# Two stores cut into 112 + 8 + 8 rows to shift packets between DMA engines, with a target for each waiting copy

## The chip, the cores and the metric

One core of one Trainium2 chip runs the kernel. The metric is device time in microseconds (us), the median of several executions. A profile of one execution is about 1.8 us shorter than the time, because it starts with the first instruction and ends with the last (before: 128.05 us for an execution with a span of 126.2 us).

## The reference

Linear attention with ReLU features: batch 8, 12 heads (96 heads in all), 512 positions, 64 dimensions, fp32.

```python
Q_feat, K_feat = np.maximum(0, Q), np.maximum(0, K)
KV = np.einsum('bhkd,bhkv->bhdv', K_feat, V)
K_sum = np.sum(K_feat, axis=2)
numerator = np.einsum('bhqd,bhdv->bhqv', Q_feat, KV)
denominator = np.einsum('bhqd,bhd->bhq', Q_feat, K_sum)
out = numerator / (denominator[:, :, :, None] + 1e-10)
```

Three inputs of 12.6 MB are read and one output of 12.6 MB is written; there is little arithmetic.

## The kernel before

The kernel works in 12 "octets" of eight heads. GpSimd issues the loads of K, V and Q ahead, two K and two V tiles and one Q tile per octet, cast to bf16 on the way (octet 0's K and V come uncast, from SP and ScalarE). SP issues the stores, one of 1 MB (128 partitions x 8 KB) per octet, and holds each of the first seven back with a tiny copy that must wait for a K tile five octets ahead: so loads go before stores. The last octet's store is cut into two halves by columns.

```python
    scratch = consts.tile([1, D], bf16, name="scratch")
    ...
    def store(o, o_sb):
        if o + DELAY < NO:                      # NO = 12, DELAY = 5
            nc.sync.dma_start(out=scratch, in_=k_sb[2 * (o + DELAY)][0:1, 0, :])
        parts = 2 if o == NO - 1 else 1
        n = RQ // parts
        for j in range(parts):
            rs = slice(n * j, n * (j + 1))
            nc.sync.dma_start(out=Or[o].rearrange("p (r d) -> p r d", d=D)[:, rs], in_=o_sb[:, rs])
    ...
    for o in range(NO + 1):                     # cut: matmuls, evacuations and preparation
        if o > 0:
            mm_out(o - 1, 2)
            norm(o - 1, 2, o_sb)
            store(o - 1, o_sb)
```

## Time and profile before

| | before |
|---|---|
| time, median of the first three runs | 127.86 us (127.86 to 128.26) |
| span of the profiled execution | 126.2 us |
| DVE, ACT, PE busy | 64%, 61%, 61% |
| DMA engines | 90% or more in 38 of 40 slices |
| last landing of the last store, per engine | eight at 122.8 to 124.0, eight at 124.6 to 125.3 us |
| last store issued | 120.05 us |

How to read it: no compute engine is near its limit, the DMA engines are. Each store of 128 rows raises its semaphore 16 times (13 of 13 stores in this trace), read here as once for each of the 16 DMA engines: while the last eight landings are still out, the DMA share is 0.46 (124.0 to 124.5 us), about eight engines of 16. So a transfer's sixteen landings in the trace show how far apart the engines are, though not which engine is which. The lines of the page and of the tail's windows are in the prediction.

### The profile page before, as it was taken

Reading aid. Unit: us, or ns where it says so; the run is one execution under the profiler, and the core shown is the slowest. Engines: PE = TensorE matmul, PEld = TensorE weight load, DVE = VectorE, ACT = ScalarE, POOL = GpSimd, SP = SyncE. Lnnn points to the kernel's source line nnn. Section 1 sums busy time; section 2 is a strip of 40 time slices with the busy share of each in tenths; the row PEclk is TensorE's granted clock in tenths of the full one; section 3 lists DMA queues with packets and bytes.
Section 4 is the critical chain, followed back from the end, with each engine's and each line's share of the span. In section 5 each row is a group of like instructions: output and inputs, shape, how many; then the busy total and the mean of one; then the engine's idle time right before and its main releaser. Section 6 shows DMA issues by size and latency. Waiting matters only on the chain.

```text
span 126.2 us, 4865 instructions
## 1 busy us (share of the span) xinstructions
PE 77.3 (61%) x2112; PEld 68.3 (54%) x2112; DVE 80.6 (64%) x210; ACT 76.9 (61%) x169; POOL 32.1 (25%) x62
## 2 busy tenths in 40 slices
PE   0032917978397956534997647389964793797200
PEld 0041907967386845434986646178953692696100
DVE  3256785698936959673669787528828628774900
ACT  0165891599198798660799949508917925958000
POOL 6902424325243331241143133033113000000000
PEclk9999999999859999996799999955999679769995
DMA  3999999999999999999999999999999999999992
GB/s 106 374 309 213 214 208 209 217 206 218 205 215 209 208 214 324 257 216 325 256 215 301 280 214 281 301 212 214 347 235 216 316 266 216 352 418 410 416 384 104
DMA packets 10757, 32.81 MB, mean 260 GB/s; under 512 B 1392, under 2 KB 1392, under 8 KB 9328
## 3 DMA queue, kind: packets, MB, share of 16 engines
q0 software_dynamic: 8064, 17.83, 73.9%
q1 hardware_dynamic: 2384, 13.63, 27.1%
q10 hardware_dynamic: 288, 1.05, 2.1%
q8 instruction: 16, 0.26, 0.7%
q14 instruction: 5, 0.04, 0.1%
HBM read 37.75 MB, written 12.58 MB: 399 GB/s over the span
## 4 chain that ended last, share of the span: by engine, by line
DMA 32%; PE 27%; issue 13%; ACT 11%; DVE 10%; ACTq 1%; SPq 0%
DMA v_sb<-in_V_dram 25%; PE ps_out L174 13%; PE ps_kv L139 11%; DMA kv_first<-in_K_dram 7%; ACT kvd L146 5%; ACT qt L159 4%; PE ps_qt L153 3%; DVE o_sb L187 3%; DVE qt L121 3%; ACT vo L134 3%; DVE kf L128 2%; DVE vo L130 1%; DVE rec L186 1%; ACTq L267 0%; DVE kvd L118 0%
## 5 line engine op out<-in xcount | busy, mean ns | idle before, releaser
L139 PE MATMUL ps_kv<-vo,kf 128*128 128x130 bf16 x384 | 32.5, 248 | 21.9 <-ACT vo L134 11.7
L174 PE MATMUL ps_out<-kvd,qt 128*32 128x130 bf16 x1536 | 33.7, 243 | 16.7 <-issue 13.3
L139 PEld LDWEIGHTS <-kf 128*128 128x128 bf16 x384 | 27.8, 112 | 25.3 <-DVE vo L130 16.3
L174 PEld LDWEIGHTS <-qt 128*32 128x32 bf16 x1536 | 27.0, 107 | 21.9 <-issue 15.3
L146 ACT CAST kvd<-ps_kv 64x130 bf16<-64x130 f32 x96 | 25.2, 263 | 16.7 <-PE ps_kv L139 14.8
L134 ACT ACTIVATE vo<-v_sb,mask 128x1024 bf16<-128x1024 bf16 x22 | 26.2, 1190 | 13.9 <-DMA v_sb<-in_V_dram 13.8
L187 DVE TENSOR_TENSOR o_sb<-ps_out,rec 128x768 f32<-128x768 f32 (+1 forms) x36 | 31.3, 868 | 1.4
L159 ACT ACTIVATE qt<-ps_qt 128x512 bf16<-128x512 bf16 x48 | 24.8, 603 | 0.3
L128 DVE TENSOR_SCALAR kf<-k_sb,mask 128x1024 bf16<-128x1024 bf16 x44 | 19.1, 476 | 8.6 <-DMA k_sb<-in_K_dram 8.6
L85 POOL DMA_DIRECT2D k_sb<-in_K_dram x22 | 12.8, 583 | 39.1 <-DMA q_sb<-in_Q_dram 24.1
L184 DVE TENSOR_SCALAR den<-ps_out 128x12 f32<-128x12 f32 (+1 forms) x36 | 5.9, 164 | 17.9 <-PE ps_out L174 17.8
L153 PE MATMUL ps_qt<-ident,q_sb 128*128 128x128 bf16 x192 | 15.7, 245 | 2.4 <-issue 2.4
L87 POOL DMA_DIRECT2D v_sb<-in_V_dram x22 | 12.3, 557 | 17.1 <-DMA k_sb<-in_K_dram 7.3
L153 PEld LDWEIGHTS <-q_sb 128*128 128x128 bf16 x192 | 14.0, 112 | 2.6 <-issue 2.5
L130 DVE TENSOR_SCALAR vo<-v_sb,mask 128x1024 bf16<-128x1024 bf16 x22 | 10.6, 481 | 2.1 <-DMA v_sb<-in_V_dram 2.1
L186 DVE RECIPROCAL rec<-den 128x12 f32<-128x12 f32 (+1 forms) x36 | 7.9, 220 | 1.2
L91 POOL DMA_DIRECT2D q_sb<-in_Q_dram x12 | 6.5, 542 | 7.8 <-DMA v_sb<-in_V_dram 4.1
L128 DVE TENSOR_SCALAR kf<-kv_first,mask 128x1024 bf16<-128x1024 f32 x4 | 2.8, 750 | 4.9 <-DMA kv_first<-in_K_dram 4.9
L134 ACT ACT_TABLE_LOAD x1 | 1.3, 1283 | 5.8 <-DMA kv_first<-in_V_dram 5.8
L121 DVE MEMSET qt<- 128x2048 f32 x2 | 3.5, 1765 | 0.8 <-issue 0.8
L134 ACT ACTIVATE vo<-kv_first,mask 128x1024 bf16<-128x1024 f32 x2 | 2.4, 1180 | 2.6 <-DMA kv_first<-in_V_dram 2.6
L130 DVE TENSOR_SCALAR vo<-kv_first,mask 128x1024 bf16<-128x1024 f32 x2 | 1.5, 747 | 0.0
(12 smaller groups left out, 3.5 us busy)
## 6 DMA issues: line engine op xcount, KB each, us to landing
out_dram<-o_sb SPq DMA_DIRECT2D x11, 1024.0 KB, 9.2
q_sb<-in_Q_dram POOLq DMA_DIRECT2D x12, 512.0 KB, 14.9
k_sb<-in_K_dram POOLq DMA_DIRECT2D x22, 256.0 KB, 13.8
v_sb<-in_V_dram POOLq DMA_DIRECT2D x22, 256.0 KB, 13.2
kv_first<-in_V_dram ACTq DMA_DIRECT2D x2, 512.0 KB, 7.3
kv_first<-in_K_dram SPq DMA_DIRECT2D x2, 512.0 KB, 7.0
out_dram<-o_sb SPq DMA_DIRECT2D x2, 512.0 KB, 5.1
scratch<-k_sb SPq DMA_DIRECT2D x7, 0.1 KB, 5.1
```

Source lines behind the costliest of these rows:

```text
L85: nc.gpsimd.dma_start(out=k_sb[g].rearrange("p r d -> p (r d)"), in_=Kr[g])
L87: nc.gpsimd.dma_start(out=v_sb[g].rearrange("p r d -> p (r d)"), in_=Vr[g])
L128: nc.vector.tensor_scalar(kf[g][:, :, s, :], k_sb[g], scalar1=0.0, scalar2=mask[:, 0, s:s + 1], op0=Alu.max, op1=Alu.mult)
L130: nc.vector.tensor_scalar(vo[g % NB][:, :, 0, 0:D], v_sb[g], scalar1=mask[:, 1, 0:1], scalar2=None, op0=Alu.mult)
L134: nc.scalar.activation(vo[g % NB][:, :, 1, 0:D], v_sb[g], Act.Copy, scale=mask[:, 1, 1:2])
L139: nc.tensor.matmul(ps_kv[g], kf[g][:, r, :, :].rearrange("p s d -> p (s d)"), vo[g % NB][:, r, :, :], start=(r == 0), stop=(r == R - 1), s ...
L146: nc.scalar.copy(kvd[g % NK][64 * c:64 * c + 64, :, s, c, :], ps_kv[g][64 * s:64 * s + 64])
L153: nc.tensor.transpose(ps_qt[o, i][:, u, :], q_sb[o][:, i * (U // 2) + u, :], ident)
L159: nc.scalar.activation(qtz[o % NZ][:, z, us, :, z, :], pv[:, :, :, z, :], Act.Relu)
L174: nc.tensor.matmul(po[hs, b, c:c + 2 * D1], qtf[o % NZ][:, z, u * P + 32 * w:u * P + 32 * w + 32], kvd[(2 * o + h // 4) % NK][:, h % 4 // ...
L186: nc.vector.reciprocal(rec, den)
L187: nc.vector.tensor_tensor(o_sb[:, 2 * u0:2 * (u0 + nu)].rearrange("p (b r) d -> p b r d", b=2), pv[:, :, :, 0:D], rec.unsqueeze(3).to_broa ...
```

## The change

Intent: the DMA engines don't end together, so two stores are cut such that eight engines carry a packet more each per store and eight one less. The tiny waiting copies get a target each, and in octets 0 to 3 there is a second one that waits for a V tile.

```diff
-    scratch = consts.tile([1, D], bf16, name="scratch")
+    scratch = consts.tile([1, 2 * NO, D], bf16, name="scratch")
...
+    def cuts(o):
+        rows = slice(0, RQ)
+        if o in (1, 3):
+            return [(slice(0, 112), rows), (slice(112, 120), rows), (slice(120, P), rows)]
+        if o == NO - 1:
+            return [(slice(0, P), slice(0, RQ // 2)), (slice(0, P), slice(RQ // 2, RQ))]
+        return [(slice(0, P), rows)]
...
     def store(o, o_sb):
-        if o + DELAY < NO:
-            nc.sync.dma_start(out=scratch, in_=k_sb[2 * (o + DELAY)][0:1, 0, :])
-        (one or two stores by columns)
+        n = 2 * (o + DELAY)
+        if n < 2 * NO:
+            for x, i in ((v_sb, n - 1), (k_sb, n))[0 if o < 4 else 1:]:
+                nc.sync.dma_start(out=scratch[:, i], in_=x[i][0:1, 0, :])
+        Ov = Or[o].rearrange("p (r d) -> p r d", d=D)
+        for ps, rs in cuts(o):
+            nc.sync.dma_start(out=Ov[ps, rs], in_=o_sb[ps, rs])
```

More of the change, by code (lines that the diff above doesn't have):

```diff
@@ L190, in norm @@
             rec.unsqueeze(3).to_broadcast([P, 2, nu, D]), op=Alu.mult)
-    def store(o, o_sb):
-        if o + DELAY < NO:
-            nc.sync.dma_start(out=scratch, in_=k_sb[2 * (o + DELAY)][0:1, 0, :])
-        parts = 2 if o == NO - 1 else 1
-        n = RQ // parts
-        for j in range(parts):
-            rs = slice(n * j, n * (j + 1))
-            nc.sync.dma_start(out=Or[o].rearrange("p (r d) -> p r d", d=D)[:, rs], in_=o_sb[:, rs])
+    def cuts(o):
[5 more added lines that the diff above has]
+        return [(slice(0, P), rows)]
+    def store(o, o_sb):
+        n = 2 * (o + DELAY)
[5 more added lines that the diff above has]
+            nc.sync.dma_start(out=Ov[ps, rs], in_=o_sb[ps, rs])
     zero(0)
```

## The prediction

The text calls eight engines "0 to 7" and the other eight "8 to 15". Take the numbers as names for two groups: those on which a transfer of 8 rows lands, and the rest. That both pieces of 8 rows take the same eight engines, one row each, was taken for granted when it was written. The trace of the kernel after agrees with it: the 112 rows of octet 1 land 16 times (61.00 to 62.63 us), the two pieces eight times each (61.59 to 63.05 and 62.21 to 63.67 us; in order, the second's are 0.50 to 0.68 us behind the first's), besides one landing each 0.44 to 0.48 us after the issue.

> **What bounds the kernel now.** I read the page first for the share of each engine, then its DMA lines, then the windows of the last stretch, and last the landings of single transfers in the trace.
>
> The busiest compute engine (DVE) is busy for 64% of the span. The DMA lines read otherwise:
>
> ```profile
> DMA  3999999999999999999999999999999999999992
> DMA packets 10757, 32.81 MB, mean 260 GB/s; under 512 B 1392, under 2 KB 1392, under 8 KB 9328
> q0 software_dynamic: 8064, 17.83, 73.9%
> q1 hardware_dynamic: 2384, 13.63, 27.1%
> q8 instruction: 16, 0.26, 0.7%
> HBM read 37.75 MB, written 12.58 MB: 399 GB/s over the span
> ```
>
> Thirty-eight of forty slices have the 16 DMA engines at 90% or more, and the queues' shares sum to 103.9% (packets overlap a little at their ends). So the transfers set the time: the kernel ends when the DMA engines have worked off their packets. The last line says how much: 50.3 MB. The q8 line will matter: 16 packets of 0.26/16 MB = 16 KB each, instruction fetches, and each runs on one engine alone.
>
> The question for this change is whether all 16 engines finish together. The windows of the tail answer it (columns: window, its length, busy time and count of PE, PEld, DVE, ACT, POOL, then granted clock, DMA share, GB/s):
>
> ```profile
> 118.00:120.00 2.00, 0.36 (x28) 0.18 (x15) 1.90 (x4) 0.00 (x0) 0.00 (x0) 1.00 0.98 403
> 121.00:122.00 1.00, 0.00 (x0) 0.00 (x0) 0.00 (x0) 0.00 (x0) 0.00 (x0) 1.00 1.03 426
> 122.00:122.50 0.50, 0.00 (x0) 0.00 (x0) 0.00 (x0) 0.00 (x0) 0.00 (x0) 1.00 0.90 361
> 122.50:123.00 0.50, 0.00 (x0) 0.00 (x0) 0.00 (x0) 0.00 (x0) 0.00 (x0) 0.76 0.68 279
> 123.00:123.50 0.50, 0.00 (x0) 0.00 (x0) 0.00 (x0) 0.00 (x0) 0.00 (x0) 0.50 0.63 254
> 123.50:124.00 0.50, 0.00 (x0) 0.00 (x0) 0.00 (x0) 0.00 (x0) 0.00 (x0) 0.50 0.52 213
> 124.00:124.50 0.50, 0.00 (x0) 0.00 (x0) 0.00 (x0) 0.00 (x0) 0.00 (x0) 0.50 0.46 188
> 124.50:125.00 0.50, 0.00 (x0) 0.00 (x0) 0.00 (x0) 0.00 (x0) 0.00 (x0) 0.50 0.09 33
> ```
>
> Compute is over at about 120 us. The DMA share is full until 122, then falls to a plateau of about one half from 123.5 to 124.5, then to nothing: about half the engines run out of work some 2 us before the rest. The trace's landings say it per engine: every store raises its semaphore 16 times, once per engine. For the last half store these times are 122.76, 122.79, 122.81, 122.83, 122.94, 123.41, 123.53, 123.97, and then 124.56, 124.93, 124.95, 124.97, 124.99, 125.08, 125.10, 125.28. Eight engines are early (mean 123.1), eight late (mean 125.0): a gap of 1.9 us. The cause fits q8. Its packets start at 25.0, 31.4, 37.4, 43.4, 49.6, 56.0, 62.1, 68.1, 74.1 and so on to 118.6 us and take 0.88 to 0.98 us. In the loads' landings one more engine falls behind after each of the first eight; from the ninth on an engine already behind falls behind a second time (the K tile landing at 76.5 has a single engine 1 us behind the next). So the same eight engines fetch twice: 2 x 0.94 = 1.9 us, the gap.
>
> How much could balancing give at most? The missing share from 122.0 to 124.87, where the last packet ends: 0.5 x (0.10 + 0.32 + 0.37 + 0.48 + 0.54) + 0.37 x 0.88 = 1.2 us. No perfect split of the same work gives more than about 1.2 us, or 1% of 127.86.
>
> [...]
>
> **The change part by part.**
>
> 1. *Octets 1 and 3 as 112 + 8 + 8.* Engines 8 to 15 go from 8 packets to 7, engines 0 to 7 to 7 + 1 + 1 = 9. Over two octets: two packets fewer on one half, two more on the other. A packet of 8 KB: in the tail, where only stores run, one engine's landings of successive 1 MB stores are 2.45 us apart (fastest engine 112.55, 114.99, 117.44), so 2.45 / 8 = 0.306 us. The shift is 0.61 us each way, 1.22 us of the 1.9 us gap, if engines 8 to 15 are the late ones. The extra pieces add two completion packets per octet on engines 0 to 7, about 20 ns each in the trace: under 0.1 us in all. The extra issues cost SP about 0.5 us each (the issues' median is 0.53); SP waits some 9 us per octet for the next K tile, so that is hidden.
>
> 2. *Four more waiting copies (V tiles, octets 0 to 3).* V tile 2(o+5)-1 is loaded ahead of the K tile that SP waits for anyway, and lands earlier: tile 9 lands at 39.36, K tile 10 at 42.86. No store goes out later for it, beyond an issue of 0.5 us that lies in the wait for K. But each copy is split into 16 packets of 8 bytes (112 of them for seven copies in the trace, median 22 ns) with a completion each of about 20 ns: some 0.05 us of every engine per copy, 0.2 us for four at most, an estimate.
>
> 3. *A target for each copy.* The chain on SP's queue before:
>
> ```profile
> SPq L197 <- DMA k_sb<-in_K_dram: 71.9, 7, 41.3
> SPq L197 <- DMA scratch<-k_sb: 22.8, 6, 4.3
> SPq L202 <- DVE o_sb L187: 9.0, 4, 5.9
> ```
>
> SP waits 22.8 us in all for the earlier copy, because all copies write one target. But a copy lands about 5 us after its issue (47.99 for the one of 42.88) and the next K tile lands at 52.9: the wait for the copy ends first and that for K ends last. Removing it starts no store earlier. Worth 0.
>
> Sum: the late engines end at 125.28 - 0.61 + 0.2 = 124.9; the early ones at latest 123.97 + 0.61 + 0.2 + 0.1 = 124.9. The two halves meet, 0.4 us sooner. The compute tail (last store issued at 120.05, earliest landing 122.76) leaves room, and loads on the late engines land a little earlier, so it doesn't take over. 127.86 - 0.4 = 127.46, said as **127.5 us**.
>
> **Rivals.**
>
> - *The wrong half.* Nothing in this trace names an engine. If the eight late ones are 0 to 7, the change adds to them: 125.28 + 0.61 + 0.2 + 0.1, a time near 128.8. For the right half speaks only that the diff was evidently drawn for this imbalance: two packets are the shift that closes most of the gap, three would overshoot. I give the wrong half 1 in 8.
> - [...]
> - *Nothing moves.* Balance is given back by another engine's lateness: the time is the maximum of 16, and the three middle ones (123.41 to 123.97) lie in the half that gets more. Then 127.7 to 127.9. The three times of before (127.86 to 128.26) spread by as much as the expected gain.
>
> **Range and chances.** The main case (two in three) gives 127.2 to 127.7; a failed half[...] 128 to 129.5. Range 127.0 to 128.7. Faster by over 2% needs 125.3 us, twice the 1.2 us that perfect balance could give: 1%. Slower by over 2% needs 130.4[...]: 3%. The rest is within 2%: 96%.
>
> **What would show it.** Right: the last transfer's sixteen landings within about 0.7 us instead of 2.5, the DMA share near 1 until about 124 and then falling at once with no plateau at one half; the split octets' last pieces land eight times; last landing 124.7 to 125.0. SP's wait for an earlier copy gone, its wait for K and V tiles as long as both before, stores issued at the same times (43.5, 53.5, 63.5). Wrong: a gap near 3 us at the end (wrong half); [...] or 8-byte packets that cost much more than 22 ns. The prediction fails as a whole if the DMA share has dips in mid-kernel that it has not now.

## The result, and the profile after

The changed kernel took 128.11 us (127.97 to 128.47, 6 runs) against 128.02 us (127.86 to 128.26, 6 runs) for the kernel before: ratio 1.0013, 95% interval 0.9994 to 1.0032. In a second set of runs, with the experiments, it was 0.9999 (0.9984 to 1.0013). So the time stayed, and the forecast gain of 0.4 us did not come.

The page of the kernel after, in the lines that answer to those of before:

```profile
DMA  3999999999999999999999999999999999999992
DMA packets 10917, 32.82 MB, mean 260 GB/s; under 512 B 1552, under 2 KB 1552, under 8 KB 9488
q0 software_dynamic: 8064, 17.83, 73.9%
q1 hardware_dynamic: 2544, 13.63, 27.1%
q8 instruction: 16, 0.26, 0.7%
```

There are 160 more packets, all under 512 bytes (64 of 8 bytes, and 96 completions: 64 of the copies, 32 of the extra pieces), and no measurable time in them: q1 takes 27.1% as before. The tail's windows, columns as before (window, length, five engines, granted clock, DMA share, GB/s):

```profile
121.00:122.00 1.00, 0.00 (x0) 0.00 (x0) 0.00 (x0) 0.00 (x0) 0.00 (x0) 0.78 0.99 410
122.00:122.50 0.50, 0.00 (x0) 0.00 (x0) 0.00 (x0) 0.00 (x0) 0.00 (x0) 0.50 0.96 393
122.50:123.00 0.50, 0.00 (x0) 0.00 (x0) 0.00 (x0) 0.00 (x0) 0.00 (x0) 0.50 1.05 426
123.00:123.50 0.50, 0.00 (x0) 0.00 (x0) 0.00 (x0) 0.00 (x0) 0.00 (x0) 0.50 0.81 328
123.50:124.00 0.50, 0.00 (x0) 0.00 (x0) 0.00 (x0) 0.00 (x0) 0.00 (x0) 0.50 0.68 279
124.00:124.50 0.50, 0.00 (x0) 0.00 (x0) 0.00 (x0) 0.00 (x0) 0.00 (x0) 0.50 0.23 90
124.50:125.00 0.50, 0.00 (x0) 0.00 (x0) 0.00 (x0) 0.00 (x0) 0.00 (x0) 0.50 0.12 49
```

Read the DMA share, the last column but one. The plateau at one half is gone: the share is high until 123 and down to 0.23 at 124. But then it does not end. From 124.5 to 125 it is 0.12, and 0.12 x 16 is two engines. The landings of the last store in the trace say the same (us):

```
before  122.76 .79 .81 .83 .94 123.41 .53 .97 | 124.56 .93 .95 .97 .99 125.08 .10 .28
after   123.49 .56 .58 .61 .69 124.05 .19 .43 .46 .47 .63 .69 .73 .89 | 125.40 .43
```

Fourteen engines are now within 1.4 us of each other, which is the balance that was meant, and two come 0.5 us behind all others. The kernel waits for those two. A second profiled execution of the changed kernel, taken with the experiments, shows the same with three: thirteen engines by 124.47, then 125.20, 125.22 and 125.55.

SP's waits in the kernel after (engine and line, what it waited for, us in total, times, longest):

```profile
SPq L210 <- DMA k_sb<-in_K_dram: 45.6, 7, 9.0
SPq L210 <- DMA v_sb<-in_V_dram: 45.4, 4, 38.3
SPq L278 <- DMA out_dram<-o_sb: 3.8, 3, 1.4
```

The wait for an earlier copy (22.8 us before) is gone, and the waits for K and V tiles took its place. The first three stores go out when they did: 43.6, 53.7, 63.6 us against 43.5, 53.5, 63.5.

### The profile page after: what moved, and what is told of

Same layout as the page of the kernel before. It is cut to its first block, busy times and chain, and to the rows that moved or that the text cites. A ratio compares the mean times of both kernels' runs of the same rounds, so it can differ in the third digit from the quotient of the medians.

```text
span 126.3 us, 4883 instructions
## 1 busy us (share of the span) xinstructions
PE 77.8 (62%) x2112; PEld 68.8 (54%) x2112; DVE 80.8 (64%) x210; ACT 77.2 (61%) x169; POOL 31.4 (25%) x62
## 3 DMA queue, kind: packets, MB, share of 16 engines
q1 hardware_dynamic: 2544, 13.63, 27.1%
## 4 chain that ended last, share of the span: by engine, by line
PE 42%; DMA 21%; issue 17%; DVE 9%; ACT 4%; ACTq 1%; SPq 0%
PE ps_out L174 18%; PE ps_kv L139 18%; DMA v_sb<-in_V_dram 14%; DMA kv_first<-in_K_dram 7%; PE ps_qt L153 6%; DVE qt L121 3%; ACT kvd L146 2%; DVE o_sb L187 2%; DVE kf L128 2%; ACT qt L159 1%; ACT vo L134 1%; DVE vo L130 1%; ACTq L278 1%; DVE rec L186 1%; DVE kvd L118 0%
## 5 line engine op out<-in xcount | busy, mean ns | idle before, releaser
L139 PE MATMUL ps_kv<-vo,kf 128*128 128x130 bf16 x384 | 33.7, 252 | 22.1 <-ACT vo L134 10.5
L139 PEld LDWEIGHTS <-kf 128*128 128x128 bf16 x384 | 28.3, 113 | 25.7 <-DVE vo L130 15.6
L184 DVE TENSOR_SCALAR den<-ps_out 128x12 f32<-128x12 f32 (+1 forms) x36 | 6.0, 166 | 22.9 <-PE ps_out L174 22.8
```

Of the source, the lines that this page charges most:

```text
L139: nc.tensor.matmul(ps_kv[g], kf[g][:, r, :, :].rearrange("p s d -> p (s d)"), vo[g % NB][:, r, :, :], start=(r == 0), stop=(r == R - 1), s ...
```

## The experiments

The theories: **A**, the late engines are just engines 8 to 15 and the gain was eaten by something else (packets, compute); **B**, the late engines are a mixed set, so that a cut by engine number makes some late ones later; **C**, it was the wrong half. Beside them stood the rival: slow packets in the small stores. The first two kernels measure which engines are late; then each part of the change runs alone; the other eight runs test what the findings predict, one of them being the changed kernel once more.

### Which engines are late: probes in both kernels

In the traces a transfer of 8 or 4 rows lands as often as it has rows, read here as on as many engines: the pieces of 8 rows eight times (above), the 8-row probe below eight times, the 4-row probe four times, each time 0.18 to 0.19 us behind a landing of the 8-row probe, so on four of the same engines. No trace numbers them: "0 to 7" are the eight of the one, "0 to 3" the four of the other, "8 to 15" the rest. That pieces and probe take the same eight is the assumption; the landings of the two pieces (above) and the shift measured below (1.3 us, 1.22 worked out) agree with it. So tiny copies behind octet 9's store report when their engines are done with it, 0.2 us later (below). The same edit was made to both kernels:

```diff
+    probe = consts.tile([16, 8, D], bf16, name="probe")
+    # behind octet 9's store
+    for i, n in enumerate((8, 4, 12, 6, 10)):
+        nc.sync.dma_start(out=probe[0:n, i], in_=ident[0:n, 0:D])
```

> A measuring kernel: the kernel before, with five tiny probe copies (8, 4, 12, 6 and 10 rows) issued right behind octet 9's store. [...] Theory A (the eight late engines are exactly 8 to 15): all eight landings of the 8-row probe lie in the early group (about 117.4 to 119.1 us), and the 12-row probe adds four late ones (near 120.0). Theory B (the late eight are a mixed set): the 8-row probe has one to three landings near 120.0 among the early ones. Theory C (wrong half): all eight near 120.0. Time at most 0.5 us over before.

Measured in the kernel before (one execution, 128.15 us, state unknown, so only the order of the engines is used):

```
store of octet 9, 16 engines   117.45 .49 .53 .81 118.02 .55 .58 119.07 | 119.21 .60 120.03 .04 .06 .08 .11 .12
probe of 8 rows (engines 0-7)  117.68 .69 .99 118.73 .77 119.40 .81 120.29
probe of 4 rows (engines 0-3)  117.88 118.18 .92 .95
```

The 8-row probe was issued first; matched in order, each of its landings is 0.2 us behind one of the store's. Less 0.2, engines 0 to 7 read 117.5, 117.5, 117.8, 118.5, 118.6, 119.2, 119.6 and 120.1: the last three are among the store's eight late landings. The 4-row probe has none of the late. So five late engines are in 8 to 15, three are in 4 to 7, and three engines of 8 to 15 are early. Theory B. (The landings of the other three probes are left out. They fit this map but for one of the 12-row probe, at 119.45, which has no store landing 0.2 us before it. The eighth and ninth landings of the store, 119.07 and 119.21, are close, so it may be the ninth that belongs to engines 8 to 15: then six late ones are there and two in 4 to 7. The set is mixed either way.)

> The same five probes in the changed kernel. Octet 9's store there lands in three groups in the profile: two early (117.1, 117.5), twelve between 118.1 and 119.8, two late (120.5). Theory B (mixed set): the two late landings belong to engines 0 to 7 (they are in the 8-row probe), which were late before and were given two packets more, and the two earliest to engines 8 to 15 (not in the 8-row probe). Theory D (something random, such as one more fetch, made two engines late): the two latest need not be among 0 to 7.

In the changed kernel (one execution, 128.71 us, state unknown):

```
store of octet 9, 16 engines   116.81 117.22 | 117.86 118.10 .11 .57 .78 119.01 .02 .16 .24 .27 .32 .47 | 120.16 .59
probe of 8 rows (engines 0-7)  118.07 .29 .76 .97 119.21 .67 120.37 .80
```

Less 0.2, the 8-row probe ends with 120.17 and 120.60: the two latest engines are both in 0 to 7. It begins with 117.87: the two earliest are both in 8 to 15. That is what moving packets from one half to the other does to a mixed set. The shift itself was the planned one. Between the two runs the latest of 0 to 7 went from 120.1 to 120.6, the five late ones of 8 to 15 from about 120.1 down to 119.0 to 119.3. Averaged over its eight engines, the first half is 0.5 us later and the second 0.9 earlier: 1.3 us between the halves (before rounding), where 1.22 was worked out.

### Each part alone

```diff
 # split only: before's copies and target, and
+        if o in (1, 3):
+            return [(slice(0, 112), rows), (slice(112, 120), rows), (slice(120, P), rows)]
 # copies only: after's copies and targets, and
-        if o in (1, 3):
+        if False:
```

> Only the split of octets 1 and 3 (112 + 8 + 8); copies and their one target as in the kernel before. If the four extra copies ate the gain (0.2 us estimated, on every engine alike): 0.2 to 0.3 us under the changed kernel, ratio to before about 0.998. If a mixed set of late engines ate it: same as before within 0.1 us, two engines still last by about 0.6 us.

> Only the copies (a V tile's copy for octets 0 to 3 and a target for each), all stores whole. If small packets cost about 0.05 us per copy on every engine: 0.2 us over before (ratio 1.0015), all sixteen end times later by 0.2 us, the gap of 1.9 us as before. If copies are free: ratio 1.000. If the free targets let SP store earlier (I expected not): below 1.

| kernel | ratio to before | 95% interval | last landing | span ends | between |
|---|---|---|---|---|---|
| before | 1 | | 125.28 | 126.19 | 0.91 |
| after | 1.0013 | 0.9994 to 1.0032 | 125.43 | 126.34 | 0.91 |
| split only | 1.0047 | 1.0035 to 1.0059 | 125.36 | 126.50 | 1.14 |
| copies only | 1.0033 | 1.0018 to 1.0049 | 125.12 | 126.27 | 1.15 |

Both expected times missed: each part alone costs more than both together. In the landings the expectations fared better. In the split alone two engines come last, at 125.27 and 125.36, 0.58 us behind the rest, as the mixed set would have it and as in the changed kernel: the split does this by itself. In the copies alone the two groups of before remain (eight at 122.80 to 124.02, eight at 124.51 to 125.12), and none is 0.2 us later. The last three columns, from the profiled executions, show where the time went: between the last landing and the end of the span 0.91 us pass in before and after, but 1.14 and 1.15 with one part. The trace of the split alone has, after the last landing, a row of SP's waits for semaphores that start at 125.37, 125.43, 125.49, 125.55 and 125.61 us; the kernel before has one such, at 125.29. SP and ACT's transfers use eight semaphores in turn (in the trace before 48 landings on each, three transfers), and at the end SP waits for them one after the other, in order (there from 120.49 us on, 0.06 us apart for those that have long landed). The kernel before issues 24 such transfers, so its last store has the eighth semaphore, the end of the row. Both parts together add eight transfers, 32, and the last store is in the eighth again. One part adds four: the last store is in the fourth, and four more waits of 0.06 us each follow its landing, 0.24 us. This "ladder" is a new theory, and was tested by itself.

### The ladder: fillers

A filler is a copy of one element, issued early. Four of them shift the last store's place by four and move next to nothing.

```diff
+    filler = consts.tile([1, 8], bf16, name="filler")
+    # behind octet 0's store, 4 (or 8) times
+    nc.sync.dma_start(out=filler[0:1, i:i + 1], in_=ident[0:1, 0:1])
```

> The kernel before plus four filler copies of one element[...], early (behind octet 0's store). They move next to nothing, but shift the last store from the last of the eight semaphores that the transfers share in turn to the fourth. Theory L (ladder): at the end SP waits for these semaphores one after the other, some 60 ns each, so a last store in the fourth costs four more steps behind the last landing: 0.24 us over before (ratio 1.002), last landing unchanged near 125.3 us. Rival (transfers cost by themselves): time as before, last landing to end of the span unchanged at 0.91 us.

> The kernel before plus eight fillers instead of four: the last store is back in the last of the eight semaphores. Ladder theory: as before (ratio 1.000, within 0.1%), span end 0.91 us after the last landing, although it issues more than the kernel with four (1.0031). Rival (each filler costs something): at least 1.003.

> The split alone plus the same four fillers, so that the last store is in the last semaphore again. Theory L: 0.24 us under the split alone (which was 1.0047), so near 1.003, and the span ends 0.91 us after the last landing instead of 1.14. With the mixed late set alone: what is left, about 0 to 0.4 us over before, is the split's own cost. Rival (no ladder): as the split alone.

> The four V copies and separate targets plus four fillers, the last store in the last semaphore again. Theory L: 0.24 us under the copies alone (1.0033), so near 1.0015, of which up to 0.2 us is small packets. Rival: as the copies alone.

> The changed kernel once more, on the same chip as the other three. Its eight extra transfers leave the last store in the last semaphore, so no ladder cost. If costs add: split's own plus copies' own (about 0.1 to 0.5 us over before). On record: ratio 1.0013.

| kernel | extra transfers | ratio to before | 95% interval | last landing | landing to end |
|---|---|---|---|---|---|
| before + 4 fillers | 4 | 1.0031 | 1.0016 to 1.0045 | 125.11 | 1.15 |
| before + 8 fillers | 8 | 1.0004 | 0.9991 to 1.0018 | 125.39 | 0.90 |
| split only | 4 | 1.0047 | 1.0035 to 1.0059 | 125.36 | 1.14 |
| split + 4 fillers | 8 | 1.0007 | 0.9993 to 1.0021 | 125.07 | 0.90 |
| copies only | 4 | 1.0033 | 1.0018 to 1.0049 | 125.12 | 1.15 |
| copies + 4 fillers | 8 | 1.0005 | 0.9992 to 1.0017 | 125.18 | 0.90 |
| after, again | 8 | 0.9999 | 0.9984 to 1.0013 | 125.55 | 0.91 |

Every kernel with four extra transfers is slower than before, every one with eight is the same as before; eight fillers cost less than four. The last column shows it directly, in single executions: 1.14 or 1.15 us with four, 0.90 or 0.91 with eight. (The two probe kernels, whose last store has the fifth semaphore and three more behind it, have 1.10.) So the ladder is shown, and the parts' apparent costs were mostly this. The last landings differ by 0.3 us between executions of kernels with the same stores (125.11 to 125.39), so they are read with care. In the ratios the ladder is worth 0.0027, 0.0040 and 0.0028, or 0.35 to 0.5 us; the traces show 0.24 us of waiting (0.0019). The split with fillers was expected near 1.003 and so missed by this. Each excess is within or near the width of the intervals, but all three are on the same side; where it goes is left open. With the ladder out of the way neither part has a time of its own that these runs resolve: the split 1.0007, the copies 1.0005.

### The split, aimed at engines that are early

If B is right, packets should go to engines 0 to 3, which are all early (117.7 to 118.8 us by the 4-row probe less 0.2; the late ones are at 119.2 to 120.1). Pieces of four rows are to do that.

```diff
 # once: octet 1, and four fillers; twice: octets 1 and 3, no filler
+            return [(slice(0, 112), rows)] + [(slice(i, i + 4), rows) for i in range(112, P, 4)]
 # and a half: octet 1 as above, octet 3 with its second half of columns cut so; seven fillers
```

> The kernel before with octet 1 alone split as 112 + 4 + 4 + 4 + 4 rows (and four one-element fillers, so that the last store stays in the last semaphore). The four-row pieces run on engines 0 to 3, which the probes showed to be early, all four of them: engines 4 to 15 carry one packet less (0.31 us), engines 0 to 3 three more (0.92 us). Mixed-set theory: all eight late engines gain 0.3 us, engines 0 to 3 stay under them (122.7 to 123.6 plus 0.92 = 123.6 to 124.6), last landing 125.0, time 0.3 us under before (ratio 0.998). [...]

> The same for octets 1 and 3 (eight extra transfers, no filler needed). Engines 4 to 15 carry two packets less (late ones near 124.7), engines 0 to 3 six more (1.84 us): 122.7 + 1.84 = 124.5 to 123.6 + 1.84 = 125.4. Mixed-set theory with the maximum setting the time: last landing near 125.3, set now by engines 0 to 3, time as before (ratio 1.000), worse than the single one. Rival (mean load sets the time): 0.6 us under before.

> Octet 1 as 112 + 4 x 4 rows, octet 3 with only half its columns so split (seven fillers keep the last semaphore). Engines 4 to 15 carry 1.5 packets less (0.46 us), engines 0 to 3 4.5 more (1.38 us): late ones 124.8, engines 0 to 3 at 124.1 to 125.0. Mixed-set theory: last landing 124.9 to 125.0, 0.3 us under before (ratio 0.9975).

| kernel | median | ratio to before (127.88 us, 13 runs) | 95% interval | last landing |
|---|---|---|---|---|
| once | 127.61 us | 0.9976 | 0.9962 to 0.9989 | 124.96 |
| twice | 128.09 us | 1.0013 | 1.0001 to 1.0026 | 125.29 |
| once and a half | 127.82 us | 0.9992 | 0.9979 to 1.0005 | 125.11 |

"Once" gives the 0.3 us that was expected, with the last landing at 124.96 where 125.0 was written down (below the 125.11 to 125.39 above), and beats both kernels (the changed one had 0.9999 and 127.98 us on the same chip). "Twice" overshoots as expected: the last landing is 125.29 (125.3 was expected), and although two packets fewer are on twelve engines, the time is that of before or a little over. (That the last ones are now engines 0 to 3 was not probed.) The mean load does not set the time; the last of the sixteen does. "Once and a half" is a miss: 0.9975 was expected, which the interval leaves out, while it includes 1; its last landing is 0.1 to 0.2 us later than worked out. Why is open.

The tail of "once" (columns as before):

```profile
122.00:122.50 0.50, 0.00 (x0) 0.00 (x0) 0.00 (x0) 0.00 (x0) 0.00 (x0) 0.50 0.80 328
122.50:123.00 0.50, 0.00 (x0) 0.00 (x0) 0.00 (x0) 0.00 (x0) 0.00 (x0) 0.50 0.86 352
123.00:123.50 0.50, 0.00 (x0) 0.00 (x0) 0.00 (x0) 0.00 (x0) 0.00 (x0) 0.50 0.66 270
123.50:124.00 0.50, 0.00 (x0) 0.00 (x0) 0.00 (x0) 0.00 (x0) 0.00 (x0) 0.50 0.58 238
124.00:124.50 0.50, 0.00 (x0) 0.00 (x0) 0.00 (x0) 0.00 (x0) 0.00 (x0) 0.50 0.14 57
124.50:125.00 0.50, 0.00 (x0) 0.00 (x0) 0.00 (x0) 0.00 (x0) 0.00 (x0) 0.50 0.00 0
```

It is less even before 124 than the changed kernel's (0.58 against 0.68 from 123.5), yet its share from 124.5 is 0.00 where that has 0.12. Only the last engine counts.

The rival of slow packets falls here too. All 128 packets of 8 KB of octet 1's store took at most 322 ns, in "once" (pieces of four rows) as in the split alone (pieces of eight), and as in the whole store of the kernel before (309 to 322 ns). In "once" the four landings of a 32 KB piece lie within 0.24 to 0.40 us; with 322 ns for a packet that is at most 0.72 us for a piece or at least 45 GB/s, an estimate.

## Why the prediction was right or wrong

- **DMA sets the time, and the engines end in two groups 1.9 us apart:** right, and what all that follows rests on. That the 16 packets of 16 KB on the queue q8, which the page calls "instruction", cause the lag was inferred: they took 0.88 to 0.98 us each, and after two of them the load that ends landing at 36.64 us has two landings of 16 behind the rest (by 0.8 us), after four the one at 50.49 has four, after seven the one at 65.46 has seven, so one engine each. No run here tells which engine carries one, so this stays argued.
- **The step that failed: "if engines 8 to 15 are the late ones".** The prediction knew that no engine is named in the trace, and then allowed only the right half or the wrong half. Eight late and eight early did not mean two halves by number. The probes show five late engines in 8 to 15 and three in 4 to 7 (or six and two). The sum "the late engines end at 125.28 - 0.61 + 0.2 = 124.9" fits the fourteen engines that end by 124.89; for the late ones in 0 to 7 the sign was the other one. Two engines stand at 125.40 and 125.43, and by the probes (octet 9's store, another execution) the two latest are in 0 to 7 (forecast for the wrong half: about 126.2, so the loss was also smaller than that). With the maximum taken over both, the forecast 0.4 us became 0. The rival "Nothing moves" came nearest: it named the outcome, and that the time is the maximum of 16. But it looked to three engines of the early half, not to late ones among 0 to 7, and of the chances (two in three, 1 in 8, and 1 in 5 for the rival that is cut) next to nothing was left for it.
- **The size of the shift:** right. 0.306 us per packet, 1.22 us between the halves; the probes show 1.3.
- **The waiting copies' 0.2 us:** too high or not resolved; with the ladder removed 1.0005, 0.06 us, interval -0.1 to +0.2.
- **A target each is worth 0:** consistent with everything seen; the wait went over to K and V tiles and stores went out at the same times. It was not run by itself.
- **Compute leaves room, since loads on the late engines land a little earlier:** half right. In the profiled executions SP issued the last store at 120.79 us instead of 120.05. Of this, 0.32 us come from a load that landed later: the last octet's first V tile, for which ScalarE waited, came at 105.61 instead of 105.29, held by a single engine 0.70 us behind the other fifteen. The rest arose on TensorE: two stretches of matmuls after it took 2.68 and 1.92 us instead of 2.52 and 1.65, in a stretch at a granted clock of 0.50 that lasted until 114.7 us (before: until 112.5). The five earliest landings, 123.49 to 123.69, are 2.7 us behind that issue, the same distance as before, so they wait for compute. The two latest do not: the slowest engine's last three stores land at 122.95, 124.19 and 125.43, 1.24 us apart, which is four packets of 0.31 us, so it had no wait for compute there.
- **What was not in the sum:** the place of the last store among the semaphores. The change adds eight transfers and so pays nothing there, by which the sum was not hurt; a prediction for either part alone would have been off by 0.3 us or more.
- **Range and chances:** the time lies in the range and within 2%, as most of the weight had it, but as a claim of 0.4 us less it was wrong.

## What to carry to other kernels

Where the DMA engines are the bound, balance is decided by the last engine (here two, 0.5 us behind the other fourteen, kept the time at that of before), so find out which engines are late (a tiny transfer of 4 or 8 rows behind a store reads it off, here 0.2 us behind the store's own landings) before packets are moved; "half are late" says nothing on which. Add or take away transfers of the hardware queues with an eye on the end of the program: a last store that isn't in the last semaphore of the turn pays the remaining waits (0.06 us each here). Test a change's parts alone and together, since parts of an additive sum that don't add are the sign of a term that was not in it.
